# A two-layer streaming encoder step: lasting PSUM banks, a pinned opening, and the last tile's norm by halves of columns

## The chip, the cores and the metric

The kernel runs on one core of one Trainium2 chip. The metric is the device time of one execution in microseconds, as the median of several runs. The profile is of one further execution of the same program.

## What is computed

There are 2048 prompt frames and 64 new frames ("sample") of 1024 numbers, with 16 heads of 64. Mixer A is a softmax over a band of the own chunk and eight chunks before it; its keys and values come from the same projection as its queries and gates. Mixer B is stick-breaking attention over keys and values that are projected once from the result of A, with 2048 cached rows ahead of the new frames. All matrix products work on float32 data that is split into a high and a low part, so that each product is three matmuls.

```python
def rms_norm(x, g):
    y = xf * lax.rsqrt(jnp.mean(xf * xf, axis=-1, keepdims=True) + RMS_EPS)
    return y * g

h = rms_norm(x, g_a);  q, k, v, gate = split(h @ w_in_a, 4)
s = q @ k.T * SCALE + rel_bias          # band of 576 keys
x = x + (softmax(s) @ v * silu(gate)) @ w_out_a

k, v = split(rms_norm(x, g_kv) @ w_kv, 2)
q, gate = split(rms_norm(x, g_b) @ w_in_b, 2)
log_fail = where(mask, log_sigmoid(-z), 0)      # z = q @ k.T * SCALE
later = reversed_cumsum(log_fail) - log_fail
w = where(mask, exp(log_sigmoid(z) + later), 0)
x = x + (w @ v * silu(gate)) @ w_out_b
y = rms_norm(x, g_f)
```

## The kernel before

**Stages.** The program has four long stages. `projections` runs for A, then the band attention, then `projections` for B, then the stick-breaking attention; the output products of A (`ps_o`) run beside the last part of the band attention and behind it, those of B beside the last part of the stick-breaking attention and behind it. The four stages begin at about 0, 727, 1432 and 2040 us.

**Projections (L216 on).** There are 17 token tiles: 16 of 128 frames and one of the 64 new frames. `normed` loads a tile (`xt`), sums its squares on ScalarE (`junk`, `ss`), forms the factor (`ms` on VectorE, a power on GpSimd), scales it, turns it with eight transposes into `ps_tr`, a PSUM tile of two banks, and splits that into a high part (ScalarE) and a low part (VectorE): `x_own`, or `big` for the second half of the tokens. The weights of v come in eight row blocks of 128x512 for each half of the columns (`vraw`, two buffers); ScalarE scales each into `vwh`, VectorE forms the rest `vwl`. Then come the products `ps_v`, tile by tile, with five PSUM banks in turn, and behind both halves the jobs for k, q and the gates (`ps_t`), whose weights are `wraw`, `wh`, `wl`. One tile is normed ahead of the one whose products run. The jobs' weights use the pool `out`, which lasts for the whole program and has two buffers each for `oh` and `ol`. Cached keys are turned in `ps_c`, new keys in `ps_n`.

**Attention.** A class `Beat` deals the work in beats: in each beat one score tile `z` for 128 queries, and for earlier tiles the transposes of the weights (`wt`), which ScalarE copies as `ph` and VectorE as the rest `pl`, and the products `acc` from both. Beside them it deals late jobs (`ps_j`, with their weights `lraw`, `lwh`, `lwl`; the token rows of k through `ps_r`), and then the output tiles: their loads, the split of the gated outputs `og` into `oh` and `ol`, the products `ps_o`, the sum with the residual `xr`, and a step `done`. In B, ScalarE forms `f` from `z`, GpSimd the pairs `two`, VectorE the scan, GpSimd the weights `s`. Each kind of tile has a fixed number of buffers: in B four for `kt` and `vt` (KV), eleven for `s` (SB), five for `ph`.

**PSUM.** Every stage has its own pool of PSUM tiles, which together fill the eight banks: in projections `ps_tr` 2, five for products, one for `ps_n`; in attention A `z` 4, `wt` and all work beside 3, `acc` 1; in attention B `z` 2, `wt` 3, `acc` 2 and one lasting constant.

**Order.** Every instruction is issued through a small wrapper at line 89, which is why most rows of the profile say L89. The order on each engine comes from a scheduler, except where the wrapper's switch `order.on` is set: there the instructions keep the order of the program. SyncE's queue issues most transfers, and ScalarE's the weights `wraw`; a transfer that waits for its buffer holds up those behind it in the queue.

**Final norm.** `done_b` (L1200 on) runs when both halves of an output tile are summed: squares of 1024 columns on ScalarE, factor, one VectorE instruction that multiplies by the factor and the weights `gf`, and one store. Output tiles are dealt in the order in which `summed` adds them, the new frames' tile at the end.

## Time and profile before

| | |
|---|---|
| median of 3 runs | 3326.24 us (3325.57 to 3326.41) |
| the profiled execution | 3318.66 us, its span 3316.9 us |
| mean granted TensorE clock | 0.992 |
| instructions in the profile | 53520 |

The span runs from the first to the last instruction; the rest of the execution's 3318.66 us lies around it. The page lists each engine's busy time (PE is TensorE, PEld its weight loads, DVE VectorE, ACT ScalarE, POOL GpSimd, SP SyncE). A row of the timeline gives start, length, engine, line, operation, what it writes and reads, shapes, and in brackets how long the engine stood before it and what released it. A name such as `ps_v` is that of a tile in the program.

### The profile page before, as it was taken

What the parts mean: (1) busy time and instruction counts of PE and PEld (TensorE: products, weight loads), DVE (VectorE), ACT (ScalarE), POOL (GpSimd) and SP (SyncE); (2) the same over time, 40 slices, a digit from 0 to 9 for tenths busy, and PEclk for the clock granted to TensorE, in tenths of its full rate; (3) what the DMA queues carried; (4) which work ended last, traced back from release to release, by engine and by line L of the source; (5) the groups of instructions that cost most, each with busy time, mean ns of one, the idle gap of its engine ahead of it and who ended that gap; (6) DMA issues with size and microseconds to landing.
All of it is one profiled execution on the core that took longest, in us unless ns stands there. A gap on an engine that the chain in (4) does not pass through costs nothing.

```text
span 3316.9 us, 53520 instructions
## 1 busy us (share of the span) xinstructions
PE 3214.8 (97%) x17928; PEld 2795.3 (84%) x17928; DVE 1916.7 (58%) x3831; ACT 1723.0 (52%) x3730; POOL 1282.8 (39%) x1933
## 2 busy tenths in 40 slices
PE   8999999999899999999999999999999989999998
PEld 7889999988788898878889998888877878888777
DVE  3324431117787776322034333999988888888873
ACT  5323322227897777233134433666766666666651
POOL 2001120005575544011043200444467776777760
PEclk9999999999999999999999999999999999999999
DMA  5449994258889894634399857677635564355523
GB/s 185 147 172 359 344 336 143 92 186 245 237 244 254 230 250 134 200 127 140 111 349 351 292 185 224 193 199 201 188 101 133 158 186 125 122 142 141 134 87 121
DMA packets 457065, 644.35 MB, mean 194 GB/s; under 512 B 49829, under 2 KB 272069, under 8 KB 456790
## 3 DMA queue, kind: packets, MB, share of 16 engines
q1 hardware_dynamic: 397334, 589.80, 57.6%
q10 hardware_dynamic: 59456, 51.13, 4.8%
q8 instruction: 143, 2.34, 0.3%
q14 instruction: 132, 1.08, 0.1%
HBM read 389.90 MB, written 250.90 MB: 193 GB/s over the span
## 4 chain that ended last, share of the span: by engine, by line
PE 81%; DVE 8%; ACT 4%; DMA 4%; issue 2%; POOL 1%; SPq 0%; POOLq 0%; ACTq 0%; DVEq 0%
PE ps_t L89 25%; PE ps_v L89 11%; PE ps_o L89 11%; PE acc L89 10%; PE z L89 8%; PE wt L89 8%; PE ps_j L89 6%; DVE s L89 3%; DVE pl L89 3%; PE ps_tr L89 1%; ACT ph L89 1%; ACT s L89 1%; DVE lwl L89 1%; DMA q<-q_a 1%; PE ps_n L89 0%
## 5 line engine op out<-in xcount | busy, mean ns | idle before, releaser
L89 DVE TENSOR_TENSOR pl<-wt,ph 128x512 fp32r<-128x512 f32 (+1 forms) x864 | 551.5, 654 | 106.2 <-ACT ph L89 103.2
L89 ACT ACTIVATE ph<-wt 128x512 fp32r<-128x512 f32 (+1 forms) x864 | 483.9, 577 | 201.4 <-PE wt L89 193.0
L89 PE MATMUL ps_t<-x_own,wh 128*128 128x362 f32 (+1 forms) x2304 | 570.2, 328 | 0.0
L89 PE MATMUL wt<-ident,s 128*128 128x128 f32 x3472 | 551.6, 275 | 12.5 <-DVE pl L89 9.0
L89 PEld LDWEIGHTS wt<-ident,s 128*128 128x128 f32 x3472 | 420.7, 141 | 87.9 <-DVE pl L89 15.1
L89 ACT ACTIVATE f<-z 128x512 f32<-128x512 f32 (+4 forms) x680 | 355.4, 536 | 185.3 <-PE z L89 122.2
L89 POOL TENSOR_TENSOR s<-f,s 128x256 f32<-128x256 f32 x416 | 360.6, 868 | 133.6 <-DVE s L89 126.3
L89 PEld LDWEIGHTS ps_t<-x_own,wh 128*128 128x128 f32 x2304 | 404.8, 188 | 1.9
L89 PE MATMUL acc<-ph,vt 128*128 128x512 f32 (+3 forms) x1088 | 376.1, 380 | 9.9 <-ACT ph L89 6.7
L89 PE MATMUL z<-kt,q 128*128 128x512 f32 (+3 forms) x1280 | 372.0, 380 | 10.0 <-ACT f L89 8.1
L89 PE MATMUL acc<-pl,vt 128*128 128x512 f32 (+3 forms) x1088 | 364.1, 368 | 17.4 <-DVE pl L89 16.6
L89 PE MATMUL ps_t<-x_own,wl 128*128 128x362 f32 (+1 forms) x1152 | 377.2, 327 | 0.0
L89 POOL TENSOR_SCALAR s<-s,rc 128x640 f32<-128x640 f32 (+5 forms) x264 | 195.9, 749 | 424.2 <-DMA keys<-k_a 250.5
L89 PE MATMUL ps_o<-big,oh 128*128 128x512 f32 x1088 | 336.9, 393 | 4.4 <-ACT oh L89 4.4
L89 DVE TENSOR_TENSOR_SCAN s<-two,s,own 128x256 f32<-128x256 f32 x408 | 299.2, 737 | 35.9 <-POOL two L89 31.7
L89 POOL TENSOR_TENSOR two<-f 128x256 f32<-128x256 f32 x416 | 262.2, 633 | 135.8 <-ACT f L89 117.9
L89 PE MATMUL ps_t<-big,wh 128*128 128x512 f32 x896 | 278.5, 391 | 0.0
L89 PEld LDWEIGHTS z<-kt,q 128*128 128x128 f32 x1280 | 221.7, 191 | 40.9 <-ACT f L89 16.9
L89 PEld LDWEIGHTS ps_o<-big,oh 128*128 128x128 f32 x1088 | 202.7, 188 | 46.7 <-ACT oh L89 5.8
L89 PEld LDWEIGHTS acc<-pl,vt 128*128 128x128 f32 x1088 | 195.2, 191 | 53.1 <-DVE pl L89 38.1
L89 PEld LDWEIGHTS acc<-ph,vt 128*128 128x128 f32 x1088 | 198.0, 191 | 34.6 <-ACT ph L89 13.2
L89 PEld LDWEIGHTS ps_t<-x_own,wl 128*128 128x128 f32 x1152 | 216.3, 188 | 0.1
(146 smaller groups left out, 5536.3 us busy)
## 6 DMA issues: line engine op xcount, KB each, us to landing
vt<-v_b SPq DMA_DIRECT2D x80, 512.0 KB, 4.8
v_b<-vs SPq DMA_DIRECT2D x64, 512.0 KB, 4.8
q<-q_a SPq DMA_DIRECT2D x128, 256.0 KB, 5.8
q<-q_b SPq DMA_DIRECT2D x128, 256.0 KB, 4.2
vt<-v_a SPq DMA_DIRECT2D x48, 512.0 KB, 7.5
kt<-k_b SPq DMA_DIRECT2D x96, 256.0 KB, 6.6
keys<-k_a SPq DMA_DIRECT2D x80, 256.0 KB, 6.0
v_a<-vs ACTq DMA_DIRECT2D x32, 512.0 KB, 2.9
```

The source lines that it names most:

```text
L89: ins = op(*args, **kwargs)
```

## The change

It has six parts.

1. A pool `turned` with three PSUM banks lasts for the whole program. `bank(name)` takes the next of them. `ps_tr`, `ps_c`, `ps_n`, `ps_j`, `ps_r`, `ps_o`, `ps_e` and `wt` all use it; `ps_tr` is now two tiles of four transposes.
2. The opening of each projections stage is written in its own order, with `order.on` set: tile 0 loaded, normed and turned, then two row blocks of the weights, tile 0 split, two more blocks, tile 1 turned, two more, tile 1 split, the last two. Tiles are turned two ahead (`xt` has four buffers). Weights of v come by two row blocks at a time, in buffers of `oh` and `ol`. The weights of the first two jobs are held until the first copy of the second half of the columns.
3. `done_b` works by halves of 512 columns: the squares of a half when that half is summed, the multiplication by `gf` apart from the factor, the factor applied to one half on ScalarE and to the other on GpSimd, and two stores.
4. The new frames' output tile is dealt one place ahead of the last, in A and in B, so that the last is a tile of 128 frames.
5. `Beat.end`, which deals the last beats of an attention stage, sets the rate at which work is dealt beside them to 1.0.
6. In attention B: five buffers for `kt` and `vt`, ten for `s`, four for `ph`.

```diff
+    turned_ps = ctx.enter_context(tc.tile_pool(name="turned", bufs=1, space=PSUM))
+    def bank(name):
+        return turned_ps.tile([P, CH], F32, name=name, tag="wt", bufs=3)
...
-                def normed(t, scale=gps.tensor_scalar):
+                def turned(t, scale=gps.tensor_scalar):
                     r0, n = TOK[t]
-                    xt = pool.tile([P, D], F32, name="xt", tag="xt", bufs=3)
+                    xt = pool.tile([P, D], F32, name="xt", tag="xt", bufs=4)
                     nc.sync.dma_start(xt[:n], x_of(t))
                     junk = pool.tile([P, D], mybir.dt.bfloat16, name="junk", tag="junk", bufs=1)
                     r = rstd_of(pool, xt, n, junk)
                     scale(xt[:n], xt[:n], r[:n], 1.0, ALU.mult, ALU.mult)
-                    ps = psum.tile([P, NK, P], F32, name="ps_tr", tag="tr", bufs=1)
-                    for k in range(NK):
-                        flip(ps[:, k, :n], xt[:n, k * P : (k + 1) * P])
+                    halves = []
+                    for k0 in range(0, NK, 4):
+                        ps = bank("ps_tr").rearrange("p (k t) -> p k t", k=4)
+                        for k in range(4):
+                            flip(ps[:, k, :n], xt[:n, (k0 + k) * P : (k0 + k + 1) * P])
+                        halves.append(ps[:, :, :n])
+                    return halves
+                def parted(t, halves):
+                    r0, n = TOK[t]
                     hf, c = spot(r0)
-                    split(*(x[:, :, c : c + n] for x in xs[hf]), ps[:, :, :n])
+                    for k0, ps in zip(range(0, NK, 4), halves):
+                        split(*(x[:, k0 : k0 + 4, c : c + n] for x in xs[hf]), ps)
                     if n == NS:
                         x_new.append(opool.tile([P, NK, P], F32R, name="x_new", tag="ol", bufs=2))
                         for i in range(2):
                             gps.tensor_copy(x_new[0][:, :, i * NS : i * NS + NS], f32(x_own[i][:, :, NEW:]))
+                def two_blocks(half, j):
+                    raw = opool.tile([P, 2, CH], F32, name="vraw", tag=("oh", "ol")[j % 2], bufs=2)
+                    c = cv + half * CH
+                    src = w_v[2 * j * P : (2 * j + 2) * P, c : c + CH]
+                    nc.sync.dma_start(raw, src.rearrange("(k p) c -> p k c", p=P))
+                    for i in range(2):
+                        k = 2 * j + i
+                        h_ = pool.tile([P, CH], F32R, name="vwh", tag=f"vwh{k}", bufs=1)
+                        l_ = pool.tile([P, CH], F32R, name="vwl", tag=f"vwl{k}", bufs=1)
+                        act.activation(h_, raw[:, i], AF.Copy, scale=gv[:, k : k + 1])
+                        dve.scalar_tensor_tensor(l_, raw[:, i], gv[:, k : k + 1], f32(h_), ALU.mult, ALU.subtract)
+                        wh.append(h_)
+                        wl.append(l_)
...
-                normed(seq[0], dve.tensor_scalar)
-                begin()
+                first_copy = None
                 for half in range(2):
                     wh, wl = [], []
-                    for k in range(NK):
-                        raw = pool.tile([P, CH], F32, name="vraw", tag="vraw", bufs=2)
-                        c = cv + half * CH
-                        nc.sync.dma_start(raw, w_v[k * P : (k + 1) * P, c : c + CH])
-                        h_ = pool.tile([P, CH], F32R, name="vwh", tag=f"vwh{k}", bufs=1)
-                        l_ = pool.tile([P, CH], F32R, name="vwl", tag=f"vwl{k}", bufs=1)
-                        act.activation(h_, raw, AF.Copy, scale=gv[:, k : k + 1])
-                        dve.scalar_tensor_tensor(
-                            l_, raw, gv[:, k : k + 1], f32(h_), ALU.mult, ALU.subtract
-                        )
-                        wh.append(h_)
-                        wl.append(l_)
+                    if half == 0:
+                        order.on = True
+                        tile0 = turned(seq[0], dve.tensor_scalar)
+                        begin()
+                        two_blocks(0, 0)
+                        parted(seq[0], tile0)
+                        two_blocks(0, 1)
+                        tile1 = turned(seq[1])
+                        two_blocks(0, 2)
+                        parted(seq[1], tile1)
+                        two_blocks(0, 3)
+                        order.on = False
+                    else:
+                        for j in range(NK // 2):
+                            two_blocks(1, j)
                     for i, t in enumerate(seq):
                         r0, n = TOK[t]
-                        if half == 0 and i + 1 < len(TOK):
-                            normed(seq[i + 1])
+                        if half == 0 and i + 2 < len(TOK):
+                            parted(seq[i + 2], turned(seq[i + 2]))
...
+                            copied = act.activation(vn[:n], out, AF.Copy)
+                            if half and first_copy is None:
+                                first_copy = copied
...
-                        nc.scalar.dma_start(raw, w[:, c : c + P].rearrange("(k p) c -> p k c", p=P))
                         wh = opool.tile([P, NK, P], F32R, name="wh", tag="oh", bufs=2)
                         wl = opool.tile([P, NK, P], F32R, name="wl", tag="ol", bufs=2)
-                        scaled_split(wh, wl, raw, g)
+                        with tc.issue_after(first_copy.ins) if j == 0 and hp < 2 else nullcontext():
+                            nc.scalar.dma_start(raw, w[:, c : c + P].rearrange("(k p) c -> p k c", p=P))
+                            scaled_split(wh, wl, raw, g)
...
-        ps = psum.tile([P, CH], F32, name="ps_c", tag="tr", bufs=1)
+        ps = bank("ps_c")
...
-            wt = psum.tile([P, CH], F32, name="wt", tag="wt", bufs=banks["wt"])
+            wt = bank("wt")
...
-                st["ps"] = psum.tile([P, CH], F32, name="ps_j", tag=banks["fo"], bufs=banks[banks["fo"]])
+                st["ps"] = bank("ps_j")
...
-        def finish():
-            done(t, n, st["xr"])
+        def finish(c):
+            done(t, n, st["xr"], c)
         products = [partial(some, c, k0) for c in range(0, D, CH) for k0 in range(0, NK, STEP)]
         cuts = [partial(cut, k0) for k0 in range(0, NK, NK // 2)]
-        return [in_place(x) for x in [load] + cuts], products, [[partial(out, 0)], [partial(out, CH), finish]]
+        return [in_place(x) for x in [load] + cuts], products, [[partial(out, c), partial(finish, c)] for c in range(0, D, CH)]
...
+            self.rate = 1.0
...
-        banks.update(wt=3, fo="wt", ph=4)
+        banks.update(ph=4)
...
-            beat.beside += out_steps("a", g, psum, w_out, x_rows, done_a)
+            at = -1 if g == GROUPS and len(beat.beside) > 1 else len(beat.beside)
+            beat.beside[at:at] = out_steps("a", g, w_out, x_rows, done_a)
...
-        KV, SB = 4, 11
-        banks.update(wt=3, fo="wt", ph=5)
+        KV, SB = 5, 10
+        banks.update(ph=4)
...
+        squares = {}
+        def done_b(t, n, xr, c):
+            i, half = c // CH, xr[:n, c : c + CH]
+            junk = pool.tile([P, CH], mybir.dt.bfloat16, name="junk", tag="junk", bufs=2)
+            if i == 0:
+                squares[t] = pool.tile([P, 2], F32, name="ss", tag="ss", bufs=4)
+            ss = squares[t]
+            act.activation(junk[:n], half, AF.Square, scale=D**-0.5, accum_out=ss[:n, i : i + 1])
+            if i:
+                ms = pool.tile([P, 1], F32, name="ms", tag="ms", bufs=4)
+                dve.tensor_scalar(ms[:n], ss[:n, 0:1], ss[:n, 1:2], EPS, ALU.add, ALU.add)
+                r = pool.tile([P, 1], F32, name="rstd", tag="rstd", bufs=4)
+                gps.tensor_tensor(r[:n], ms[:n], nhalf[:n], ALU.pow)
+            dve.tensor_tensor(half, half, gf[:n, c : c + CH], ALU.mult)
+            if i == 0:
+                return
             dst = o["y_s"] if t == 16 else o["y_p"][t * P : (t + 1) * P]
-            nc.sync.dma_start(dst, xr[:n])
+            act.activation(xr[:n, :CH], xr[:n, :CH], AF.Copy, scale=r[:n])
+            gps.tensor_scalar(xr[:n, CH:], xr[:n, CH:], r[:n], 1.0, ALU.mult, ALU.mult)
+            for x in range(0, D, CH):
+                nc.sync.dma_start(dst[:, x : x + CH], xr[:n, x : x + CH])
```

The same replacement as for `ps_j` is made for `ps_r`, `ps_n`, `ps_o` and `ps_e`, the functions lose their argument `psum`, and `summed` of B is changed as that of A.

The orders on the engines, of before and of the change, at the places that the prediction speaks of:

ScalarE at the start of the program, before (`wh` and `wraw` are weights of the first job, `vwh` and `vraw` of v, `junk` the squares of a token tile, `x_own` its high part, `g_a` the norm weights):

```order
L307 DMA wraw<-in_w_in_a 128x8x128
L89 ACT_TABLE_LOAD
L89 ACTIVATE junk,ss<-xt 128x1024
L89 ACTIVATE wh<-wraw,g_a 128x128 x8
L89 ACTIVATE vwh<-vraw,g_a 128x512 x2
L89 ACTIVATE junk,ss<-xt 128x1024
L89 ACTIVATE x_own_155<-ps_tr 128x8x128
L89 ACTIVATE junk,ss<-xt 128x1024 x2
```

and with the change:

```order
L89 ACT_TABLE_LOAD
L89 ACTIVATE junk,ss<-xt 128x1024
L89 ACTIVATE vwh<-vraw,g_a 128x512 x2
L89 ACTIVATE x_own_158<-ps_tr 128x4x128 x2
L89 ACTIVATE vwh<-vraw,g_a 128x512 x2
L89 ACTIVATE junk,ss<-xt 128x1024
L89 ACTIVATE vwh<-vraw,g_a 128x512 x2
L89 ACTIVATE junk,ss<-xt 128x1024 x2
L89 ACTIVATE x_own_158<-ps_tr 128x4x128 x2
L89 ACTIVATE vwh<-vraw,g_a 128x512 x2
```

The transfer `wraw` and the eight instructions that make `wh` are gone from this place, and the four pairs of `vwh` stand between the squares and the copies of tiles 0 and 1, which are halves now.

ScalarE in the first beats of the band attention, before (`sp` is the high part of a late job's k, `ph` the copy of turned weights, `s` the exponentials, `lkn` the token rows of k):

```order
L89 ACTIVATE ph<-wt 128x512
L89 ACTIVATE s,sm<-s,mn 128x128
L89 ACTIVATE sp<-ps_j 128x512
L89 ACTIVATE ph<-wt 128x512
L89 ACTIVATE s,sm<-s,mn 128x256
L89 ACTIVATE lkn<-ps_r 128x512
```

and with the change:

```order
L89 ACTIVATE ph<-wt 128x512
L89 ACTIVATE s,sm<-s,mn 128x128
L89 ACTIVATE ph<-wt 128x512
L89 ACTIVATE s,sm<-s,mn 128x256
L89 ACTIVATE sp<-ps_j 128x512
L89 ACTIVATE lkn<-ps_r 128x512
```

`ph` and `s` of the next beat have moved ahead of `sp`.

VectorE where the output tiles of A end and the projections of B begin, before (`xr` is a sum with the residual; the two steps over `ol` are those of the new frames' tile; `ms` belongs to a token tile's factor):

```order
L89 TENSOR_TENSOR xr<-ps_o,xr 128x512 x2
L89 TENSOR_TENSOR ol<-ol,xr 64x512
L89 TENSOR_TENSOR xr<-ps_o,ol 64x512
L89 TENSOR_TENSOR ol<-ol,xr 64x512
L89 TENSOR_TENSOR xr<-ps_o,ol 64x512
L89 TENSOR_TENSOR x_own_15656<-ps_tr,x_own_15655 128x8x128
L89 TENSOR_SCALAR ms<-ss 128x1
```

and with the change:

```order
L89 TENSOR_TENSOR ol<-ol,xr 64x512
L89 TENSOR_TENSOR xr<-ps_o,ol 64x512
L89 TENSOR_TENSOR ol<-ol,xr 64x512
L89 TENSOR_TENSOR xr<-ps_o,ol 64x512
L89 TENSOR_TENSOR xr<-ps_o,xr 128x512 x2
L89 TENSOR_SCALAR ms<-ss 128x1
L89 TENSOR_SCALAR xt<-xt,rstd 128x1024
L89 SCALAR_TENSOR_TENSOR vwl<-vraw,g_kv,vwh 128x512 x2
L89 TENSOR_TENSOR x_own_15694<-ps_tr,x_own_15693 128x4x128 x2
L89 SCALAR_TENSOR_TENSOR vwl<-vraw,g_kv,vwh 128x512 x2
```

The new frames' tile has moved one place ahead, and the first tile's `ms`, its scaling, and `vwl` of the first two blocks stand behind the last `xr` and ahead of the low part of tile 0; before, the low part stood right behind `xr`, and the scaling and `vwl` of these stood further ahead in the queue.

SyncE's queue when the stick-breaking attention begins, before (`kt` and `vt` are loads of keys and values, `gate_b` is the store of a late job's gates `sg`, `gt` a load of gates):

```order
L467 DMA vt<-v_b 128x4x256
L89 DMA lraw<-in_w_in_b 128x8x128
L461 DMA kt<-k_b_116 64x2x512 x2
L467 DMA vt<-v_b 128x4x256
L446 DMA q<-q_b_108 64x2x512 x2
L452 DMA gt<-gate_b_125 128x512
L503 DMA kt<-k_b_116 128x2x64
L685 DMA gate_b_125<-sg 128x512
```

and with the change:

```order
L503 DMA vt<-v_b 128x4x256
L89 DMA lraw<-in_w_in_b 128x8x128
L497 DMA kt<-k_b_119 64x2x512 x2
L503 DMA vt<-v_b 128x4x256
L721 DMA gate_b_128<-sg 128x512
L482 DMA q<-q_b_111 64x2x512 x2
L488 DMA gt<-gate_b_128 128x512
L539 DMA kt<-k_b_119 128x2x64
```

The store gate_b<-sg has moved from behind the second pair of `vt`, `q`, `gt` and `kt` to right behind `vt`.

71 lines of the change are left out of this document (34 added, 37 removed).

## The prediction

> **What bounds the kernel now.** I read the page's busy table and the chain that ended last first, to see which engine sets the time.
>
> ```profile
> PE 3214.8 (97%) x17928; PEld 2795.3 (84%) x17928; DVE 1916.7 (58%) x3831; ACT 1723.0 (52%) x3730; POOL 1282.8 (39%) x1933
> PE 81%; DVE 8%; ACT 4%; DMA 4%; issue 2%; POOL 1%; SPq 0%; POOLq 0%; ACTq 0%; DVEq 0%
> ```
>
> TensorE works 3214.8 of 3316.9 us. The change leaves its matmuls and transposes alone, so only the other 102.1 us, and stretches at a lower granted clock, can shrink. Windows of 5 us over the whole span show where they lie; these are the ones at the places that the change touches. Columns: window, length, then busy time and count for PE, PEld, DVE, ACT, POOL, then granted clock, DMA share, GB/s.
>
> ```profile
> 5.00:10.00 5.00, 1.97 (x8) 1.57 (x8) 0.91 (x2) 3.63 (x12) 0.55 (x1) 1.00 1.06 331
> 10.00:15.00 5.00, 2.03 (x6) 1.35 (x7) 2.85 (x5) 4.51 (x8) 2.39 (x4) 1.00 0.86 224
> 755.00:760.00 5.00, 1.21 (x8) 0.71 (x6) 0.00 (x0) 0.36 (x1) 3.71 (x5) 0.83 0.65 204
> 760.00:765.00 5.00, 4.23 (x19) 4.23 (x20) 3.38 (x10) 4.09 (x12) 1.31 (x3) 0.50 1.00 243
> 1325.00:1330.00 5.00, 3.85 (x17) 3.20 (x18) 1.67 (x4) 1.40 (x3) 0.32 (x1) 1.00 0.65 217
> 1435.00:1440.00 5.00, 3.71 (x15) 2.62 (x13) 1.22 (x1) 1.32 (x2) 0.00 (x0) 0.50 0.53 151
> 2070.00:2075.00 5.00, 1.42 (x8) 1.18 (x8) 2.27 (x5) 1.65 (x5) 0.97 (x3) 0.74 0.90 301
> 2715.00:2720.00 5.00, 3.52 (x16) 3.46 (x17) 1.93 (x4) 0.93 (x2) 2.08 (x4) 0.50 1.09 371
> ```
>
> A gap can cost twice: PE stands, and behind some gaps (near 757, 1434, 2072 and 2714) the clock is lower for some us; behind that of 1326 it is not. What stands ahead of each gap comes from the timeline (start, length, engine, operation; idle before it and what released it).
>
> **The change, term by term.**
>
> 1. *First opening.*
>
> ```profile
> 7.39 1.97 PE L89 MATMUL ps_tr<-ident,xt 128*128 128x128 f32 x8 [7.39 <-DVE xt L89]
> 7.03 2.45 ACT L89 ACTIVATE wh<-wraw,g_a 128x128 fp32r<-128x128 f32 x8 [1.37 <-DMA g_a<-in_norm_a]
> 9.38 1.32 ACT L89 ACTIVATE vwh<-vraw,g_a 128x512 fp32r<-128x512 f32 x2
> ```
>
> PE cannot begin before 7.39 (tile 0 must land and be scaled), and the change leaves that. From 9.36 to 15 it stands 5.64 − 2.03 = 3.6 us, because ACT, in its order, spends 2.45 us on weights of a job that runs 200 us later before it splits the first v weights. The change holds those back and puts vwh first. Against that, v weights come in 512 KB pieces, so the first lands later, and eight vwh and the copies of two tiles share ACT. I take −3.0: 2.45 plus part of the transfer that goes. Bounds: 0 (the first piece lands as late as wh ended) and −3.6 (all idle behind 9.36).
>
> 2. *Banks between stages.*
>
> ```profile
> 729.14 0.74 PE L89 MATMUL ps_j<-big,lwh 128*128 128x512 f32 x2 [1.62 <-ACT sg L89]
> 2042.31 0.73 PE L89 MATMUL ps_j<-big,lwh 128*128 128x512 f32 x2 [2.18 <-DVE sl L89]
> ```
>
> Both are the first late job of an attention stage, which waits until the projections' last evacuation frees the bank that it inherits. In the lasting pool its bank was last used by transposes further back, so both waits go: −1.6 and −2.1. What is late next, z's own banks, has the same origin; bounds 0 and −3.8 together.
>
> 3. *ACT's queue at 755 and SP's behind it.*
>
> ```profile
> 757.61 0.66 PE L89 MATMUL ps_r<-ident,lkn 128*128 128x128 f32 x4 [2.06 <-POOL lkn L89]
> 759.64 0.60 ACT L89 ACTIVATE sp<-ps_j 128x512 fp32r<-128x512 f32 x1 [5.33 <-DMA k_a<-sp]
> 760.77 0.79 PE L89 MATMUL acc<-ph,vt 128*128 128x256 f32 x2 [2.51 <-ACT ph L89]
> ```
>
> ACT waits 5.33 us to write sp again until the transfer k_a<-sp has read it, and ph, which acc needs, stands behind. Now ph and s stand ahead of sp, so the 2.51 us need not recur; the 2.06 us on POOL's lkn stay. What comes late next is z, by the row after: s of 0.51 us still behind ph. −2.0; bounds 0 (sp only delays lkn, and with it ps_r) and −5.9 (the 3.79 us that PE stands from 755 to 760, and half of the 4.23 busy us at 0.50).
>
> 4. *End of band attention.*
>
> ```profile
> 1326.14 1.20 PE L89 MATMUL ps_o<-big,oh 128*128 128x512 f32 x4 [2.52 <-ACT oh L89]
> ```
>
> ACT's oh<-og stood behind the copies of the sample's totals, which wait for DVE. In the new order it stands ahead of them, and with the rate at 1.0 more ps_o are dealt among the last beats. −2.0; bounds 0 and −2.5.
>
> 5. *Second opening.*
>
> ```profile
> 1427.83 3.79 PE L89 MATMUL ps_o<-big,oh 128*128 128x512 f32 x16
> 1433.07 0.68 DVE L89 TENSOR_TENSOR xr<-ps_o,ol 64x512 f32<-64x512 f32 x1
> 1433.96 1.83 PE L89 MATMUL ps_tr<-ident,xt 128*128 128x128 f32 x8 [2.34 <-issue]
> 1436.96 0.80 PE L89 MATMUL ps_v<-vwh,x_own 128*128 128x512 f32 x1 [1.16 <-ACT x_own L89]
> L89 DVE TENSOR_SCALAR xt<-xt,rstd 128x1024 f32<-128x1024 f32 x2 | 1.5, 750 | 0.7 <-POOL rstd L89 0.7
> ```
>
> The last ps_o ends at T = 1431.62; the transposes wait 2.34 us, until DVE has read the bank, and ps_v begins at T + 5.3. The lasting bank frees them, but the pinned DVE order now puts tile 0's ms and scaling behind the last xr. With rows of the tail below (xr 0.69, ms 0.15, pow 0.54) and 0.75 for the scaling, the transposes can start at T + 0.04 + 0.69 + 0.18 + 0.68 + 0.80 ≈ T + 2.4, as late as now. A wait replaces the wait. The last v weights (j = 2, 3) also wait for buffers that the last ps_o holds, and then for their transfers; tile 1, turned ahead, comes earlier than before. I take 0; bounds +3 and −3.
>
> 6. *Transfers in stick-breaking attention.*
>
> ```profile
> 2073.35 0.60 ACT L89 ACTIVATE sp<-ps_j 128x512 fp32r<-128x512 f32 x1 [3.86 <-DMA gate_b<-sg]
> 2074.49 0.69 PE L89 MATMUL z<-kt,q 128*128 128x128 f32 x2 [3.44 <-ACT f L89]
> 2716.48 1.09 PE L89 MATMUL acc<-pp,vt 128*128 128x128 f32 x4 [4.65 <-DMA vt<-v_b]
> ```
>
> At 2074 f, which frees z's bank, stands behind an sp that waits for gate_b<-sg; SP issued that store late, behind loads that waited for their buffers. With five kt/vt buffers SP's order has that store earlier. Of 3.44 I take −2.0 (bounds 0, if SP blocks on another load first; −5.2, with a half clock as behind 2716 gone too). At 2716 vt was issued late for the same reason, with DMA at 371 GB/s, so part of the wait is bandwidth: −2.5 of 4.65 (bounds 0; −6.4, with half of the 3.52 busy us at 0.50).
>
> 7. *Rings in stick-breaking attention:* ph from 5 to 4, s from 11 to 10.
>
> ```profile
> PE acc L89 <- DVE pl L89: 16.0, 42, 1.3
> L89 PE MATMUL acc<-pl,vt 128*128 128x512 f32 (+3 forms) x640 | 241.2, 393 | 16.4 <-DVE pl L89 16.0
> ```
>
> PE waits there for pl 42 times over 640 products. The regular beat holds three ph and ten s alive, so the cut only just fits: 0. Bounds: 0, since fewer buffers bring nothing forward, and, if one product in eight (80 more) waits the 16.0/42 = 0.38 us of those rows, +30.
>
> 8. *Final norm.* Each tile gains on ACT two reads of the accumulator's kind and a copy: 2×(0.60+0.19)+0.60 against 1.06+0.19, on DVE 2×0.69 against 1.28, on POOL 0.70. An out tile takes 84.00/368×48 = 11.0 us of PE (the ps_o run below), far more than ACT's 2.2 plus 2.4 for its four oh at 0.60; hidden there. Among beats ACT may not cover it wholly: 0, bounds 0 and +3 (a fifth of the 17×0.93 us more on ACT).
>
> 9. *Tail.*
>
> ```profile
> 3223.58 84.00 PE ps_o L89 x368
> L89 DVE TENSOR_TENSOR xr<-ps_o,xr 128x512 f32<-128x512 f32 x64 | 44.0, 687 | 101.5 <-PE ps_o L89 101.0 <-DMA xr<-in_x_prompt 0.3
> L89 POOL TENSOR_SCALAR s<-s,rc 128x512 f32<-128x512 f32 x16 | 11.2, 697 | 5.7 <-DVE rc L89 4.8 <-PE wt L89 0.7
> 3307.60 0.59 ACT L89 ACTIVATE ol<-ps_o 64x512 f32<-64x512 f32 x1 [3.03 <-PE ps_o L89]
> 3309.78 1.06 ACT L89 ACTIVATE junk<-xr 64x1024 bf16<-64x1024 f32 x1 [1.58 <-DVE xr L89]
> 3310.74 0.19 ACT L89 ACTIVATION_READ_ACCUMULATOR junk<-xr 64x1 f32 x1
> 3310.96 0.15 DVE L89 TENSOR_SCALAR ms<-ss 64x1 f32<-64x1 f32 x1 [1.26 <-ACT junk L89]
> 3311.25 0.54 POOL L89 TENSOR_TENSOR rstd<-ms,nhalf 64x1 f32<-64x1 f32 x1 [8.09 <-DVE ms L89]
> 3311.83 1.28 DVE L89 SCALAR_TENSOR_TENSOR xr<-xr,rstd,gf 64x1024 f32<-64x1024 f32 x1 [0.72 <-POOL rstd L89]
> 3313.13 0.51 SPq L1216 DMA_DIRECT2D out_y_s<-xr  x1
> ```
>
> The last matmul ends at 3307.56 (by 3307.60), the store is issued 5.57 later, the span ends 3.77 after that. With a 128-row tile last there is no ol step: xr 0.73, then a square of half the columns 0.08 + 0.69 (0.60 and its read), ms 0.18, pow 0.68, and halves on POOL (0.70) and ACT (0.60) side by side: 3.06, with the gaps of before; gf lies beside pow on DVE. The second store is issued 0.5 later: 3.56, against 5.57. −2.0; bounds −1.0 (half stores land later) and −2.8.
>
> Sum: −3.0 − 1.6 − 2.1 − 2.0 − 2.0 + 0 − 2.0 − 2.5 + 0 + 0 − 2.0 = **−17.2 us**. The profiled execution took 3318.66 us, which would become 3301.5; the median of the runs shown is 7.6 us higher, and 3326.24 − 17.2 = **3309.0**.
>
> **A rule weighed.** Behind the 2.34 us gap at 1433.96 the clock was 0.50 in the next five us, behind the 2.52 us gap at 1326.14 it was 1.00; between the last ps_o and the first ps_v at 1436.96, which is no transpose, lie 5.34 us. The Trainium skill, "TensorE: Matmul & The Clock Gate", says in Part 1: The HAM clock gate that PE falls to half rate after an idle window of about 3.4 us, and in Part 4: PE-mode transpose that transposes do not count as busy in the same way; the trace agrees at both places if both hold together. By these, term 5 stays as it is (ps_v still begins some 5 us behind T), while at 760, where only the transposes ps_r would stand between two shorter gaps, the half clock would go with the wait: 2.2 us more, and a sum of −19.4. No row shows such a place with ph on time, so I leave term 3 at the gap alone.
>
> **Rivals.**
> - *A, slower: the rings are too short.* Only if s or ph comes free later than the next beat needs it. The 42 waits on pl say that ACT and DVE are sometimes just late there; against it, PE waits 16.0 us in all, so there is slack in most beats. It decides from 17.2/0.38 = 45 more such waits, one in 14 products; at one in eight it costs 30 and gives 3309.0 + 30 = 3339.
> - *B, within 0.2%: queues only trade places.* The waits on ACT and SP (terms 1, 3, 4, 6) turn into others behind the next slow transfer, as the beats keep their rate; banks and tail stay, −3.7 − 2.0 = −5.7: 3320.5. For it: term 5 is such a trade already. The change not doing what it says belongs here: if ps_j's lasting bank was used last by a late transpose, 2.0 is left, 3324.
> - *C, more: gaps and their half clock go together:* the far bounds of terms 1, 3, 4, 6 with banks and tail, −3.6 − 5.9 − 2.5 − 11.6 − 5.7 = −29.3: 3297.
>
> **How the numbers follow.** Forecast (3300 to 3319) 0.62, B 0.18, C 0.10, A 0.10. A measurement tells 0.2% (6.65 us) from no change, so faster means under 3319.6: forecast and C, 0.72; same 0.18, from B; slower 0.10, from A. The range 3298 to 3324 takes in forecast and B with the bounds of single terms, and leaves out A and about half of C.
>
> **What would show it.** Right: PE full from about 12 us on; no wait of ps_j at 729 and 2042; acc at 760 and z at 2074 without their waits; clock 1.00 at 762 and 2716; the span's end some 7.3 us behind the last matmul. Term 5: transposes 2.4 us behind the last ps_o, released by DVE xt. Wrong: PE's waits for DVE pl, or DVE's and ACT's for buffers, grown by more than 17 us between 2070 and 3215; new gaps of a few us in the openings, with 0.50 behind them.

## The result, and the profile after

| | before | changed |
|---|---|---|
| median | 3326.32 us (3325.57 to 3327.66, 4 runs) | 3305.14 us (3299.76 to 3307.47, 4 runs) |
| ratio, 95% interval | | 0.9932 (0.9917 to 0.9948) |
| profiled execution | 3318.66 us, span 3316.9 | 3303.79 us, span 3301.9 |

By the medians the change wins 21.2 us; the forecast was 17.2. The two profiled executions differ by only 14.9, because that of before was a quick one of its kind: in the later comparisons the kernel before took 3320.5 to 3330.0 us.

The page of the changed kernel, its busy line and the engines' shares of the chain that ended last:

```profile
PE 3215.2 (97%) x17928; PEld 2796.8 (85%) x17928; DVE 1922.0 (58%) x3882; ACT 1730.6 (52%) x3815; POOL 1296.1 (39%) x1950
PE 77%; DVE 8%; issue 5%; DMA 4%; ACT 3%; POOL 2%; SPq 1%; POOLq 0%; DVEq 0%; ACTq 0%
```

TensorE's work is the same as before (3214.8), so its time without work fell from 102.1 to 86.7 us. The windows of the changed kernel at the places shown before (the same times; the work in them has moved by up to 10 us):

```profile
5.00:10.00 5.00, 2.50 (x9) 2.07 (x10) 2.69 (x5) 2.88 (x7) 0.56 (x1) 1.00 1.00 373
10.00:15.00 5.00, 5.00 (x17) 3.72 (x16) 4.51 (x7) 4.51 (x8) 2.02 (x2) 1.00 1.00 313
755.00:760.00 5.00, 3.21 (x14) 2.92 (x15) 0.89 (x2) 1.52 (x3) 3.41 (x5) 0.50 0.73 221
1325.00:1330.00 5.00, 5.00 (x29) 4.34 (x28) 1.25 (x2) 0.32 (x1) 2.56 (x2) 1.00 0.48 141
2715.00:2720.00 5.00, 4.17 (x17) 2.41 (x17) 4.94 (x9) 4.29 (x9) 4.84 (x7) 1.00 0.25 95
```

TensorE works nearly all the time from 10 us on; near 1325 the gap is gone, and at 2715 the half clock, with a shorter gap ahead of the window. At 755 the half clock has stayed. The timeline's rows of TensorE at the waits that answer to those of before:

```profile
756.11 1.11 PE L89 MATMUL ps_r<-ident,lkn 128*128 128x128 f32 x4 [4.71 <-POOL lkn L89]
1432.16 1.09 PE L89 MATMUL ps_tr<-ident,xt 128*128 128x128 f32 x8 [2.37 <-issue]
2066.11 1.22 PE L89 MATMUL z<-kt,q 128*128 128x512 f32 x2 [5.34 <-ACT f L89]
2708.57 0.48 PE L89 MATMUL acc<-ph,vt 128*128 128x512 f32 x1 [1.48 <-DMA vt<-v_b]
```

At 2708 4.65 us have become 1.48. At 756 one wait of 4.71 us stands for two of 2.06 and 2.51, and at 2066 one of 5.34 for one of 3.44. The rows for ps_j at 729 and 2042 and for ps_o at 1326 have no counterpart: those waits are gone. The end, all engines:

```profile
3294.37 0.39 PE L89 MATMUL ps_o<-big,ol 128*128 128x512 f32 x1
3294.79 0.69 DVE L89 TENSOR_TENSOR xr<-ps_o,xr 128x512 f32<-128x512 f32 x1 [3.16 <-PE ps_o L89]
3295.58 0.63 ACT L89 ACTIVATE junk<-xr 128x512 bf16<-128x512 f32 x1 [4.67 <-DVE xr L89]
3296.63 0.92 POOL L89 TENSOR_TENSOR rstd<-ms,nhalf 128x1 f32<-128x1 f32 x1 [7.77 <-DVE ms L89]
3297.65 0.69 POOL L89 TENSOR_SCALAR xr<-xr,rstd 128x512 f32<-128x512 f32 x1
3298.33 0.81 SPq L1273 DMA_DIRECT2D out_y_p<-xr  x2
```

From the last matmul (3294.76) to the end are 7.1 us, 9.3 before.

### The profile page after: what moved, and what is told of

The parts are those of the page before. It is cut to its first block, busy times and chain, and to the rows that moved or that the text cites. A ratio compares the mean times of both kernels' runs of the same rounds, so it can differ in the third digit from the quotient of the medians.

```text
span 3301.9 us, 53682 instructions
## 1 busy us (share of the span) xinstructions
PE 3215.2 (97%) x17928; PEld 2796.8 (85%) x17928; DVE 1922.0 (58%) x3882; ACT 1730.6 (52%) x3815; POOL 1296.1 (39%) x1950
## 4 chain that ended last, share of the span: by engine, by line
PE 77%; DVE 8%; issue 5%; DMA 4%; ACT 3%; POOL 2%; SPq 1%; POOLq 0%; DVEq 0%; ACTq 0%
PE ps_t L89 25%; PE ps_v L89 11%; PE acc L89 10%; PE ps_o L89 8%; PE z L89 8%; PE wt L89 8%; PE ps_j L89 5%; DVE s L89 3%; DVE pl L89 2%; PE ps_tr L89 1%; DVE lwl L89 1%; ACT ph L89 1%; ACT s L89 1%; POOL s L89 1%; PE ps_c L89 1%
## 5 line engine op out<-in xcount | busy, mean ns | idle before, releaser
L89 PEld LDWEIGHTS z<-kt,q 128*128 128x128 f32 x1280 | 221.4, 190 | 39.9 <-ACT f L89 16.7
```

What stands on the lines that cost most here:

```text
L89: ins = op(*args, **kwargs)
```

## The experiments

To compare kernels by place, each trace was cut at the same pieces of work, and the lengths stand in this table (us). Open A: from the start to the product ps_v behind the first 36. A start, A middle and A end: from the last product of the projections of A to the 61st and the 1141st transpose of weights, and to the last ps_o of A. Open B: from there to the ps_v behind the first 36 of B. B start, middle, late and last: from the last product of the projections of B to the transposes 1441, 2401 and 2521 (counted through the whole program; A has 1160 of them), and to the last matmul. Tail: to the end of the span.

| kernel | open A | A start | A middle | A end | open B | B start | B middle | B late | B last | tail |
|---|---|---|---|---|---|---|---|---|---|---|
| before | 26.6 | 57.4 | 526.3 | 120.4 | 17.7 | 180.0 | 484.4 | 70.7 | 532.5 | 9.3 |
| changed | 22.3 | 57.3 | 529.5 | 117.7 | 15.9 | 180.1 | 482.6 | 67.7 | 530.0 | 7.1 |
| again | 22.7 | 57.5 | 534.1 | 117.7 | 16.0 | 178.7 | 482.6 | 69.2 | 530.2 | 7.1 |
| u_banks2 | 22.4 | 59.8 | 525.3 | 117.7 | 15.9 | 183.7 | 482.9 | 69.7 | 530.1 | 7.1 |
| u_rings | 22.3 | 58.3 | 531.2 | 117.7 | 16.0 | 178.7 | 486.5 | 68.8 | 530.6 | 7.1 |
| f_sg3 | 22.4 | 56.5 | 531.1 | 117.7 | 16.0 | 176.7 | 482.7 | 67.2 | 530.1 | 7.1 |
| f_both | 22.4 | 56.9 | 528.8 | 117.7 | 16.0 | 179.1 | 482.6 | 68.1 | 530.2 | 7.1 |
| u_pin | 22.4 | 59.3 | 527.5 | 117.7 | 16.7 | 179.5 | 482.6 | 67.7 | 530.0 | 7.1 |
| u_hold | 23.3 | 57.2 | 526.2 | 117.7 | 16.0 | 179.5 | 482.8 | 68.2 | 530.1 | 7.1 |
| u_rate | 22.3 | 58.2 | 532.0 | 122.0 | 16.0 | 179.2 | 482.7 | 68.4 | 530.7 | 7.1 |
| u_norm | 22.3 | 58.0 | 525.7 | 117.7 | 16.0 | 179.7 | 482.6 | 71.2 | 538.2 | 7.6 |
| u_norm_rate | 22.2 | 57.3 | 526.5 | 122.0 | 16.1 | 180.3 | 482.6 | 67.9 | 534.1 | 7.6 |
| u_place | 22.2 | 59.8 | 526.5 | 117.6 | 18.6 | 180.2 | 482.6 | 67.7 | 530.0 | 8.8 |

Where kernels have the same code in a stretch, the column shows what differs from one execution to the next: nearly nothing in A end, B middle and B last, some 2 us in B start and B late, 3 in A start, 9 in A middle. So a whole time of one execution says little here, and most verdicts below rest on a column.

**The changed kernel again** (no edit).

> The changed kernel itself once more, for its spread and for the clock. In its profile band attention has half-clock stretches at 825, 945 and 1030 us that the kernel before lacks, though the gaps there are nearly the same (0.96, 1.74, 1.78 us against 0.94, 1.74, 1.14). Theory: where the clock falls behind gaps of 1 to 2 us is a matter of each execution, so these stretches lie elsewhere or are gone here, and the time is anywhere from 3299 to 3308. Rival: they belong to the new order, come at the same three places again, and the time from 780 to 1060 us is within 0.5 us of the first profile.

3303.77 us (3298.76 to 3308.23), ratio 0.9928 (0.9913 to 0.9943). The half clock at 825 was absent in this execution, with the same gap ahead of it. The windows and the row behind them, of the first profile and then of this one:

```profile
825.00:830.00 5.00, 4.94 (x28) 4.94 (x29) 3.22 (x13) 2.79 (x9) 2.08 (x4) 0.66 0.88 264
823.46 0.73 PE L89 MATMUL z<-keys,q 128*128 128x512 f32 x2 [0.95 <-DVE mn L89]
```

```profile
825.00:830.00 5.00, 4.99 (x37) 4.57 (x38) 4.57 (x17) 4.30 (x10) 2.81 (x5) 1.00 0.67 209
823.28 0.74 PE L89 MATMUL z<-keys,q 128*128 128x512 f32 x2 [0.95 <-DVE mn L89]
```

At 945 and 1030 the half clock came again. So in this run the theory holds for one place of three. But the stretch that the rival names took 280.2 and 282.3 us between the same transposes, and in the twelve profiles of the changed kernel and its variants the half clock stands near 945 in five and near 1030 in seven: it is not a fixed cost of the new order.

**No lasting banks** (u_banks, u_banks2). A pool of three banks for each stage, behind z and acc in attention, as they lay before:

```diff
-    turned_ps = ctx.enter_context(tc.tile_pool(name="turned", bufs=1, space=PSUM))
+    turned_ps = [None]
...
         tc.tile_pool(name="band_ps", bufs=1, space=PSUM) as psum,
+        tc.tile_pool(name="turned_band", bufs=1, space=PSUM) as turned_ps[0],
```

> The change without lasting banks: three PSUM tiles in a pool of each stage, placed as in the kernel before in attention. The waits of ps_j at 727 and 2036 us come back (1.6 and 2.2 us). Theory: what was won there is given back at the next place where ScalarE or GpSimd waits for a store to land (756 and 2066 us), so those gaps shrink by about as much, and by 800 and by 2100 us the kernel is at most 1 us behind the changed one; whole time within 2 us of it. Rival, as in the prediction: both waits count in full, 3.7 us later at 2100 us than the changed kernel.

> The change without lasting banks again, for a profile at the usual clock; of the run before only times were usable. The theory and its rival stand as there: bank waits of 1.6 and 2.2 us come back at 727 and 2036, and by 800 and 2100 us the kernel is at most 1 us behind the changed one (theory: a store's landing sets the time there), or 1.6 and 3.7 us behind (rival).

The first left no profile at the usual clock, so only its times count: ratio 0.9945 (0.9926 to 0.9964). The second: 3308.13 us (3304.39 to 3309.01), ratio 0.9945 (0.9928 to 0.9961). TensorE's rows of u_banks2 at both bank waits, and what follows the second:

```profile
726.37 0.74 PE L89 MATMUL ps_j<-big,lwh 128*128 128x512 f32 x2 [1.62 <-ACT sg L89]
2034.53 0.88 PE L89 MATMUL ps_j<-big,lwh 128*128 128x512 f32 x2 [2.18 <-DVE sl L89]
2062.89 0.33 PE L89 MATMUL wt<-ident,s 128*128 128x128 f32 x1 [2.31 <-DVE sp L89]
2071.86 0.39 PE L89 MATMUL acc<-ph,vt 128*128 128x256 f32 x1 [3.21 <-ACT ph L89]
```

Both waits are back, at the length that they had before. In B start this costs 183.7 against 178.7 to 180.3 in the eight profiles with the same code there and lasting banks, 3.4 to 5 us: the rival is right there, the bank's wait counts in full and more. Why more is open. In A start u_banks2 took 59.8, as u_place did with lasting banks, and the kernel before, with its bank wait, 57.4, no more than most: that fits the theory, by which the 1.6 us are given back there, but one profile with a scatter of 3 us doesn't settle it. The rows of f_both, below, bear on it too.

**Rings of before in B** (u_rings).

```diff
-        KV, SB = 5, 10
-        banks.update(ph=4)
+        KV, SB = 4, 11
+        banks.update(ph=5)
```

> The change with the buffers of before in stick-breaking attention: four kt and vt, eleven s, five ph. Theory: the fifth vt ended the 4.65 us wait at 2716 and the half clock behind it, so a wait for vt of about 4 us and 7 to 10 us of half clock come back near 2710, and the kernel loses 4 to 6 us between 2690 and 2760; waits for pl stay at 16 to 18 us. Rival A: the shorter s and ph rings cost time, so waits for pl fall by 3 us or more and the stretch before 2690 is over 2 us shorter.

3307.04 us (3300.98 to 3313.87), ratio 0.9939 (0.9922 to 0.9956). The waits of TensorE from 2034 us on, grouped (us, times, longest), and then the row of its longest wait for a load:

```profile
PE acc L89 <- DVE pl L89: 15.7, 34, 1.3
PE acc L89 <- DMA vt<-v_b: 4.2, 1, 4.2
```

```profile
2712.05 0.63 PE L89 MATMUL acc<-pp,vt 128*128 128x128 f32 x4 [4.17 <-DMA vt<-v_b]
```

The wait for vt is back. B middle and late together are 555.3, as before (555.1), against 550.3 and 551.8 in the two profiles of the change: the new rings together are worth 3.5 to 5 us. But 3.9 of it lie in B middle, which ends at 2700.5, ahead of the wait for vt; B late, which holds that wait, is 68.8, between the 67.7 and 69.2 of the change, since its last part is shorter there. So the theory's place, 2690 to 2760, is only in part right. TensorE's longest waits in the last 100 us of B middle are these:

```profile
2605.60 0.66 PE L89 MATMUL acc<-pp,vt 128*128 128x128 f32 x4 [1.56 <-DVE pp L89]
2695.46 0.41 PE L89 MATMUL z<-kt,q 128*128 128x128 f32 x2 [1.39 <-DMA kt<-k_b]
```

Behind the first follow 3.4 us of half clock, which the kernel before, with the same wait, lacks. The run undoes all three rings at once, so what the fifth kt and vt are worth alone is not shown. Waits for pl fall from 17.4 us (40 times) and 18.4 (41) in the two profiles of the change to 15.7, less than the 3 us that the rival asked for, and the stretch ahead of 2690 isn't shorter.

**More buffers for late stores** (f_sg3 in B; f_both in A and B).

```diff
-                sg = opool.tile([P, CH], F32, name="sg", tag="xr", bufs=2)
+                sg = late_pool[0].tile([P, CH], F32, name="sg", tag="late", bufs=3)
...
-            st["kn"] = opool.tile([P, 2, CH], F32, name="lkn", tag="xr", bufs=2)
+            st["kn"] = late_pool[0].tile([P, CH], F32, name="lkn", tag="lkn", bufs=1)
...
```

(The first pair is f_sg3, both pairs are f_both.)

> The change with three buffers of their own for sg in stick-breaking attention, so that ScalarE's sp no longer waits until the store of sg has landed. Theory: the 5.34 us gap at 2066 and its 6.8 us of half clock are that wait; both go, 5 to 8 us won by 2100 us, and most of it stays to the end: some 3298 to 3300 us. Rival: the wait only passes to the next load of kt or vt, whose transfers fill the queue there; a gap of 3 us or more stays between 2055 and 2075, and less than 2 us is won.

3301.00 us (3299.74 to 3310.4), ratio 0.9930 (0.9912 to 0.9947). The 5.34 us wait is gone and no half clock is left in stick-breaking attention ahead of the last matmul; the largest wait in B start is 1.27 us, for a load of q. B start is 176.7, 2 to 3.5 us under the others with lasting banks: less than the 5 to 8 of the theory.

> The change with three buffers of their own for sg in stick-breaking attention, and with a tile of its own for the late jobs' token rows lkn in both attentions (half as large, since the turned rows are written over the source). Theory: at 756 us ps_r waits 4.7 to 6 us in the changed kernel for lkn, and lkn for the store of sp whose buffer it takes; with its own tile that gap is under 1.5 us and the 7 to 10 us of half clock behind it are gone: 5 to 9 us won by 800 us, against 57 to 60 us from the projections' end to the 61st turned weight now; with sg's 3.7 us the median is 3293 to 3298. Rival: what landed late there is not the store but the loads behind it (vt, q), and the gap passes to acc or z at the same place: under 2 us won by 800 us.

3302.02 us (3298.42 to 3305.73), ratio 0.9930 (0.9917 to 0.9944). The rival is right in the size, A start 56.9 against 57.3 and 57.5, but not in the place: the gap stays at ps_r. TensorE and ScalarE of f_both near 755, and TensorE at 2078:

```profile
755.36 1.12 PE L89 MATMUL ps_r<-ident,lkn 128*128 128x128 f32 x4 [5.94 <-DVE sp L89]
753.99 0.60 ACT L89 ACTIVATE sp<-ps_j 128x512 fp32r<-128x512 f32 x1 [6.39 <-DMA vt<-v_a]
2078.03 1.12 PE L89 MATMUL z<-kt,q 128*128 128x128 f32 x4 [2.12 <-DMA q<-q_b]
```

lkn has its own buffer, and now ScalarE's next sp waits, and with it ps_r, until about the same moment: ps_r begins 31.0 us behind the end of the projections, with the change 30.8. (ScalarE's row names a load of vt issued at 737.56; the store k_a<-sp issued at 748.02 uses the same semaphore, so it may be that store which the wait was for.) What the 20 us ahead were filled with, windows of the kernel before, the changed one and f_both show, in this order:

```profile
735.00:755.00 20.00, 19.92 (x110) 17.15 (x109) 11.61 (x36) 11.73 (x26) 4.00 (x5) 1.00 1.03 305
```

```profile
735.00:755.00 20.00, 16.33 (x93) 13.95 (x92) 11.57 (x37) 12.11 (x28) 5.00 (x7) 0.97 1.04 311
```

```profile
735.00:755.00 20.00, 14.35 (x81) 12.07 (x79) 9.56 (x31) 10.46 (x22) 6.87 (x8) 0.97 1.02 302
```

In all three the DMA engines are full (share 1.02 to 1.04, 302 to 311 GB/s). TensorE's work in them, 19.92, 16.33, 14.35 us, falls because its wait for ps_r moves into the window: it begins at 755.6, 751.4 and 749.4 and ends at 757.6, 756.1 and 755.4. Counted from the end of the projections, TensorE comes to it after 28.0, 26.1 and 25.0 us and leaves it after 30.1, 30.8 and 31.0, with a DMA share of 0.99 to 1.02 over the whole of it. So the first beats of A appear bound by their transfers, and what is won between the end of the projections and this place is waited for here; no run with fewer transfers there tests it. What is won ahead of the projections' end is not lost by it: A start is 57.3 us with the change and 57.4 before. B start of f_both, 179.1, also shows that f_sg3's gain there did not come with the same buffers for sg in another profile: 2.12 us wait there for q.

**The opening left to the scheduler** (u_pin) and **the first jobs' weights not held** (u_hold).

```diff
-                        order.on = True
...
-                        order.on = False
```

```diff
-                        with tc.issue_after(first_copy.ins) if j == 0 and hp < 2 else nullcontext():
+                        with nullcontext():
```

> The change with the opening left to the scheduler (the rest of it as changed). The first 36 ps_v end at 22.3 us with the change and at 26.6 before. Theory: the gain comes from the job's weights that no longer stand there and from two tiles turned ahead, not from the pinned order, and the scheduler puts four vwh ahead of tile 0's high part: 1 to 2 us later than the change, 23.3 to 24.3. Rival: the pinned order carries the whole gain, 26 us or later. At the second opening: the pinned order put the transposes 2.4 us behind the last ps_o; theory says left to the scheduler they come at most 0.5 us earlier, since xr, ms and the scaling are one chain there in any order; rival: 1 us or more earlier.

> The change with the weights of the first two jobs not held back. The 36th ps_v begins at 22.3 us with the change, at 26.6 before. Theory of the prediction: these weights (2.45 us on ScalarE and a transfer of 512 KB) carried the wait, so 2 us or more come back, 24.3 or later. Rival: in the new order ScalarE does not split them there even so, only the transfer is back; the two tiles ahead and the early v weights carry the gain, and it is under 23.2.

u_pin: 3304.41 us (3301.67 to 3305.33), ratio 0.9935 (0.9920 to 0.9949). Open A is 22.4, so even less is lost than the theory says; the scheduler has four vwh ahead of the high part, and it does no harm. At the second opening the theory falls: the transposes follow the last ps_o at once, 2.4 us earlier than with the pinned order. TensorE's rows:

```profile
1428.33 0.40 PE L89 MATMUL ps_o<-big,ol 128*128 128x512 f32 x1
1428.57 1.04 PE L89 MATMUL ps_tr<-ident,xt 128*128 128x128 f32 x8
1430.83 0.63 PE L89 MATMUL ps_tr<-ident,xt 128*128 128x128 f32 x4 [1.23 <-DVE xr L89]
1433.06 0.50 PE L89 MATMUL ps_v<-vwh,x_own 128*128 128x512 f32 x1 [1.60 <-ACT x_own L89]
```

The first tile of B doesn't depend on the last ps_o, since B begins with another group of frames; only the order of the queues tied them. Yet open B is 0.7 longer: here ps_v begins 4.3 us behind the last ps_o (3.7 with the change), since the high part now stands on ScalarE behind two vwh that wait for their transfer. u_hold, one time: 3301.71 us; open A 23.3, 1.1 later, between what both asked for. ScalarE's row shows what came back, a later v weight (7.46 in the changed kernel):

```profile
8.35 1.33 ACT L89 ACTIVATE vwh<-vraw,g_a 128x512 fp32r<-128x512 f32 x2 [2.63 <-DMA vraw<-in_w_in_a]
```

So of the 4.3 us of open A some 1.1 hang on the transfer of the held weights, and next to none on the pinned order alone. The other 3 were not undone: the two tiles ahead, the v weights that are all under way at once, and ScalarE's 2.45 us of wh, which stand in the opening of neither run (u_pin holds these weights, and u_hold's ScalarE has no wh in its first 24 us). No run leaves out both the pinned order and the holding.

**Rate and norm** (u_rate, u_norm, u_norm_rate).

```diff
-            self.rate = 1.0
```

```diff
+            if not c:
+                return
+            junk = pool.tile([P, D], mybir.dt.bfloat16, name="junk", tag="junk", bufs=1)
+            r = rstd_of(pool, xr, n, junk)
+            dve.scalar_tensor_tensor(xr[:n], xr[:n], r[:n], gf[:n], ALU.mult, ALU.mult)
```

(The second is done_b of u_norm, in place of the steps by halves; u_norm_rate has both.)

> The change with the final norm of before (squares of 1024 columns, one instruction for factor and weights, one store). From the last matmul to the end: 7.1 us with the change, 9.3 before. By the rows: xr 0.73, squares of 1024 columns and their chain to rstd 2.06, 1.38 for factor and weights, then 3.8 from issue to end: 8.0. The rest of the attention stays within 1 us by theory (the work on ScalarE was hidden); by the rival, that the added work on ScalarE among the beats costs, stick-breaking attention from 2600 us on is over 2 us shorter.

> The change without the rate of 1.0 in the last beats. From the 1141st turned weight of band attention to the end of the output products of A, and from the 2521st turned weight of stick-breaking attention to the last matmul (530.0 us, within 0.2, in seven profiles with the new norm and the rate; 532.5 before). Theory: without the rate the wait of ps_o for oh behind the sample's totals (2.5 us before) comes back, and the last stretch of B is again 532 to 533. Rival: the new norm and the lasting banks alone give 530, and the rate is worth under 0.5 us there.

> The change with the final norm of before and without the rate of 1.0. With the old norm and the rate the last stretch of B took 538.2 us, 8 more than the change and 6 more than before, with a wait of 3.68 us where VectorE's factor-and-weights instruction stands ahead of pp. Theory: the rate, which deals more output tiles among the last beats, brings the old norm's long instructions in the way; without both the stretch is 532 to 534, as before. Rival: the old norm costs 8 us beside the new banks and rings whatever the rate, 537 or more.

u_rate: 3309.98 us (3307.16 to 3311.23), ratio 0.9952 (0.9938 to 0.9965). A end is 122.0, 4.3 longer: the 2.52 us wait of ps_o for oh is back, and 3.4 us of half clock behind it. The row of that wait:

```profile
1329.77 1.19 PE L89 MATMUL ps_o<-big,oh 128*128 128x512 f32 x4 [2.52 <-ACT oh L89]
```

B last is 530.7: there the rival is nearly right, and the rate is worth 0.7, a little more than the 0.5 it allowed. u_norm, one time: 3311.39 us; its tail is 7.6, not 8.0, and B last 538.2, 8 us longer, where theory and rival had the attention the same or shorter. u_norm_rate, one time: 3309.22 us, B last 534.1, just past the theory's 534. The row of TensorE in u_norm, and those of VectorE and GpSimd ahead of it:

```profile
3214.70 0.44 PE L89 MATMUL wt<-ident,s 128*128 128x128 f32 x2 [3.68 <-DVE pp L89]
3212.02 2.17 DVE L89 SCALAR_TENSOR_TENSOR xr<-xr,rstd,gf 128x1024 f32<-128x1024 f32 x1
3213.19 2.14 POOL L89 TENSOR_TENSOR ot<-ot,gt 128x512 f32<-128x512 f32 x1
```

VectorE waits for squares and factor of a whole tile, then multiplies 1024 columns, and pp, which frees the bank of wt, stands behind. With the rate one more output tile falls among the last beats: nine such instructions stand ahead of the last transpose of weights, eight without it, and the row is the ninth. Behind the wait follow 3.4 us of half clock. B last is 534.1 without the rate and 538.2 with it; with halves it is 530.7 and 530.0. So the halves are worth 3.4 us in B last without the rate, lost piece by piece through the stretch, and 8.2 with it: the norm by halves is what lets the rate pay there.

**The new frames' tile last** (u_place).

```diff
-            at = -1 if g == GROUPS and len(beat.beside) > 1 else len(beat.beside)
+            at = len(beat.beside)
```

(The same line stands in A and in B.)

> The change with the new frames' tile last again, in A and in B. By the rows: behind the last matmul ol 0.64, two sums 0.77 and 0.77, then squares of a half 0.77, ms 0.18, pow 0.68, halves 0.65 and the second issue 0.5 and 3.6: 8.5 us to the end against 7.1. At the second opening the transposes come 1.4 us later, 3.8 us behind the last ps_o. Rival: the place of the tile does nothing, both as with the change within 0.4 us.

One time, 3305.60 us. The tail is 8.8 (expected 8.5), and at the second opening the wait is as expected:

```profile
1431.74 0.66 PE L89 MATMUL ps_tr<-ident,xt 128*128 128x128 f32 x2 [3.77 <-issue]
```

Open B is 18.6, 2.7 longer than with the change, for 1.4 us more of a wait. With it 6.8 us of half clock follow, with the change 3.4; but the second profile of the change has none there and took the same 16.0, so what the clock has to do with the other 1.3 us is not shown. The rival falls.

None of the kernels that were tried is clearly quicker than the changed one: f_sg3 and f_both have its ratio within the interval.

## Why the prediction was right, and where it was wrong

The time lies in the range, the sign and the size are right: 3309.0 was forecast, 3305.14 measured. That the sum came so near is in part luck. Term 3, the first half of term 6 and term 2's share in A, 5.6 us together, were not won; 1.7 at the second opening, 2.5 in B last, which both stood at 0, and 2.4 in the projections of B, which was not in the sum, made up for them. Term by term:

- *Term 1, first opening (−3.0):* open A won 4.3, of which 2.2 to 3.5 were left where the projections end (727.5 before, 724.1 to 725.3 in most profiles; 727.0 with the weights not held, where TensorE also waited 1.5 us for the loads kr at 240 and 251 us). The size is right. The reason named, 2.45 us of wh on ScalarE, stays open: not holding those weights brought back their transfer alone, for 1.1, leaving out the pinned order cost nothing, and no run put wh back in its old place.
- *Term 2, banks (−3.7):* both waits are gone. In B undoing it cost 3.4 to 5 us, more than the 2.1 forecast; why more than the wait itself is open. In A the 1.6 us came to nothing as far as the columns show (A start, which holds this wait, is 57.4 before and 57.3 and 57.5 with the change). The step that failed there is "both waits go" taken as time won.
- *Term 3, ScalarE at 755 (−2.0):* failed. ph and s moved ahead of sp as the order showed, but the wait went to lkn (4.71 us), and with a buffer for lkn back to sp. The step that failed is "the 2.06 us on POOL's lkn stay": TensorE came to that wait 4.2 us earlier than before (751.4 against 755.6) and could leave it only 1.5 earlier. That was rival B in this one place.
- *Term 4, end of band attention (−2.0):* A end won 2.7 and loses 4.3 without the rate. The size is right, and the rate carries all of it: without it the 2.52 us wait for oh stands as before, so the rest of the change did not move oh ahead by itself.
- *Term 5, second opening (0, +3 to −3):* the wait of 2.4 us for the transposes came as worked out (2.37), and it is the pinned order's, as u_pin shows. Open B still won 1.7, though the term stood at 0: ps_v began 3.7 us behind the last ps_o, not the 5.3 of before. The half clock there was 3.4 us instead of 6.8 in one profile and absent in the next, with the same length.
- *Term 6 (−2.0 and −2.5):* the first failed, as term 3: 3.44 became 5.34 us, and B start is the same (180.0, and 178.7 to 180.3). The second was about right in its place: B late, which holds the wait for vt, won 3.0 and 1.4 in the two profiles of the change, and the wait fell from 4.65 to 1.48 and 0.3. Another 1.8 was won ahead of it, in B middle, and no term named that. The half clock is gone for good only in part: of the eleven profiles with five vt, seven have 3.4 us or more of it between 2706 and 2740.
- *Term 7, rings (0; rival A):* waits for pl went from 16.0 in 42 to 17.4 in 40 times, and 18.4 in 41 in the second profile. Rival A's price was not paid.
- *Term 8, final norm (0, 0 to +3):* the mechanism was missed. The step that failed is the pair of bounds, 0 and +3, taken from ScalarE's added work: the halves cost nothing among the beats, they win, since VectorE's long instruction no longer stands ahead of pp. Taking them back costs 3.4 us in B last without the rate and 8.2 with it; the change as a whole won 2.5 there.
- *Term 9, tail (−2.0):* 9.3 became 7.1. Right: 0.4 of it from the halves, 1.7 from the tile's place, by u_norm and u_place.

A gain of 2.4 us between the second opening and the end of the projections of B, where ps_n and ps_c share three banks, was not in the sum (590.9 us before, 587.6 to 589.2 in the others); no run undid it alone. The stretches that repeat sum to about −19 us by typical values. A middle, 526.3 us in the one profile of before and 525.3 to 534.1 in the twelve others, can't be compared so; where the rest of the 21.2 by the medians lies remains open.

**The rule weighed.** The Trainium skill, "TensorE: Matmul & The Clock Gate", Part 1: The HAM clock gate, speaks of an idle window of about 3.4 us. The stretches at half clock here are 3.4, 6.8 and 10.2 us long (all but the last of each trace, which lies behind its last matmul), so the trace agrees with a window of that length; but with 0.95 us of a gap at 823 the clock fell in three of the twelve profiles since the change and not in the other nine, so a gap need not be as long as the window. Nor does the length of a gap decide: behind the 2.52 us at 1326 the clock stayed at 1.00 before, and behind the same 2.52 us in u_rate and u_norm_rate it fell for 3.4 us. So that one execution agreed with the rule at both places did not bear it out. At 755 the forecast by the rule, that the half clock goes with the wait, was not put to the test, since the wait stayed.

## What to carry to other kernels

A wait that is removed inside a stretch bound by transfers may not be time won: look at the DMA share of the next 20 us before counting it. Where a load has to wait for its buffer in a queue, one more buffer of the load can be worth more than the buffers of the intermediate tiles that pay for it; here the swap won 3.5 to 5 us as a whole. When work is dealt more densely beside other work, cut its longest instructions first, on the engine whose short ones the bound engine waits for.

## What the runs showed of the hardware

- Whether the clock halves behind a gap of 1 to 2 us changes from one execution to the next, of the same code too (at 825 us: three of twelve profiles, all with a gap of 0.94 to 0.96 us).
- The multiplication of 128x1024 on VectorE, 1.33 us on average before, took 2.17 us beside a GpSimd instruction that took 2.14 instead of 1.30 on average: at that place, working at the same time, both were slower. Not every overlap does it: at 2993.76 in the same run the multiplication took 1.27 us with GpSimd at work for 1.2 us of it.
